# Attention of a transformer block: where the batches of maxima stand among the value products, where the additions follow, how often a modulation step comes, and what is held in SyncE's order

## The chip, the cores and the metric

The kernel runs on one core of one Trainium2 chip. The time is the device time of one execution in microseconds (us). Three runs of the kernel before gave 3038.39, 3041.65 and 3044.37 us, a median of 3041.65.

## What is computed

The reference is one layer of a diffusion backbone over 2048 latent tokens and 256 context tokens, all in float32: normalised and modulated input, a combined input projection, attention and a gated branch, a merge with an output projection, and a feed-forward part. The change touches the attention alone. There are 8 query heads and 2 key heads of 64 numbers, and each query reads 2304 keys (18 tiles of 128: two of context, sixteen of latent tokens).

```
def attend(q, k, v):
    s = jnp.einsum('bkgqd,bknd->bkgqn', q, k, preferred_element_type=jnp.float32)
    p = jax.nn.softmax(s, axis=-1).astype(v.dtype)
    return jnp.einsum('bkgqn,bknd->bkgqd', p, v)
```

## The kernel before, in words

**Units.** The attention (`attend`, L1119) goes through 16 units. A unit is a block of 512 queries (`b`, four of them) and a pair of heads (`p`, four of them). Units are numbered 0 to 15 here.

**What a unit needs.** Softmax is done with the maximum of each query subtracted. So before a unit's scores, its maxima have to be known: `maxima` (L2064) multiplies the queries' high halves with all keys, and VectorE reduces each 128x512 result to a column (L2084 for context keys, L2089 for the others). One call of `maxima(3)` is called a batch here: three steps, each of which fills two banks of PSUM and has two reduces. `reference` (L2093) takes the maximum over all key tiles. `leading` (L2100) turns the result into rows on TensorE (L2104), copies them on ScalarE (L2106) and sends them with eight transfers on SyncE's queue (L2109) into the first row of the operand `qb`, so that the product that follows subtracts the maximum. `cast` (L2052) and `remainder` (L2058) split the queries of a later unit into two parts; the second is two subtractions on VectorE (L2061).

**The order within a unit.** A unit's 18 key tiles are three groups of six (`GROUP`), `gi` 0, 1, 2; the text calls the work of one pass of this loop a block. For each key tile two products of scores are made for two heads (`first`, L2123, and `second`, L2142), and ScalarE takes their exponential out of PSUM (L2146) into the buffers `p2` (eight of them) and `t4`. Then come the first batch of maxima of a later unit, the value products of the group before (`pend`, `values`, L2149, the product in L2156), and the second batch. In blocks 0 and 1 the batches are of the next unit, in block 2 of the one after it. `values` also adds the exponentials up for the softmax's sum: key tiles 2, 4, 8 and 14 on VectorE (L2169), the others on GpSimd (L2172). `leave` (L2176) copies a finished output out of PSUM (L2180), `join` (L2183) adds the two sums (L2186), `sums` (L2193) sums over the partitions with a product with ones (L2199) and `inverse` (L2209) makes the reciprocal.

**What is done beside it.** `mod_part` (L352) makes one of the modulation vectors in steps of two rows of weights, on VectorE (L386, L390), in buffers of the tag `raw`; after each half of the vector a product with ones (L417) and two instructions of VectorE finish it. It is advanced three times a unit from unit 1 on, at the fifth key tile of each group. In the last unit `late` (`br_inputs`, L1188) loads eight inputs of the branch merge, four of one branch (`gm_d`) and four of the attention (`at_d`), and splits each of them, one a key tile: a load into one of three `raw` buffers (L1198), for the attention's also a load of the inverse sums (L1202) and a product with them on VectorE (L1217), a cast on ScalarE (L149) and a subtraction on VectorE (L153).

**What sets the order.** A scheduler places the instructions of each engine. In `attend` the instructions of TensorE and VectorE keep the order in which the code is written (`self.fixed`, read by `order`). ScalarE's, GpSimd's and SyncE's do not, save that buffers of one tag are first written in the written order, and save what `self.loads` holds, a list of stretches in which SyncE's transfers keep the written order; before, nothing of the attention is in it. PSUM has eight banks, all of one tag. A unit's output holds one from its first value product to `leave`, and the rest turn among scores, maxima and sums.

Of the kernel before, what the change touches and what calls it, by code (L numbers as in the profile page):

```python
# [29 lines left out]
TB = 512  # L30
# [34 lines left out]
GROUP = 6  # L65
# [4 lines left out]
class Kern:  # L70
# [1048 lines left out]
    def attend(self, units, late, mod):  # L1119
        self.psum({"b": 8})  # L1120
        begin = self.here()
        pend = []
        for i, u in enumerate(units):
            at = lambda n: units[n] if 0 <= n < len(units) else None
            nxt, far, old, older = at(i + 1), at(i + 2), at(i - 1), at(i - 2)
            for gi, g in enumerate(range(0, NKT, GROUP)):
                group = range(g, g + GROUP)
                step = nxt if gi < 2 else far
                for j in group:
                    u.first(j)  # L1130
                    u.second(j)
                    if j % GROUP == 2 and far and gi == 0:
                        far.load()
                    if j % GROUP == 4 and nxt and gi == 2:
                        nxt.leading()
                    if not nxt:
                        next(late, None)
                    elif i and j % GROUP == 4:
                        next(mod, None)
                if step:  # L1140
                    step.maxima(3)
                for f in pend:
                    f()
                if gi == 1 and far:
                    far.cast()
                if gi == 2 and old:
                    old.sums()
                if step:
                    step.maxima(3)
                if gi == 0:  # L1150
                    if older:
                        older.inverse()
                if gi == 2 and far:
                    far.remainder()
                if gi == 1:
                    if nxt:
                        nxt.reference()
                    if old:
                        old.join()
                pend = [lambda u=u, j=j: u.values(j) for j in group]  # L1160
            pend.append(u.leave)
        for _ in mod:
            pass
        for f in pend[:-1]:
            f()
        units[-2].inverse()
        units[-1].join([self.sb("raw", [TB]) for _ in range(2)])
        self.fixed.append(range(begin, self.here()))
# [865 lines left out]
class Unit:  # L2034
# [114 lines left out]
    def values(self, j):  # L2149
        k, nc = self.k, self.nc  # L2150
        c, i, _ = self.keys(j)
        pt, whole = self.pts.pop(j)
        if j == 0:
            self.o = k.bank([TB])
        for h in range(2):
            nc.tensor.matmul(  # L2156
                self.o[h * HD : (h + 1) * HD, :], k.V[c][:, i, self.kv * HD : (self.kv + 1) * HD],
                pt[h], start=j == 0, stop=j == NKT - 1,
            )
        e = j in (LAST_ON_VECTOR if self.last else ON_VECTOR)  # L2160
        old = self.acc.get(e)
        if old is None:
            self.acc[e] = whole
            return
        if e not in self.own:
            self.own.add(e)
            self.acc[e] = k.sb("ac", [2, TB])
        if e:
            nc.vector.tensor_tensor(out=self.acc[e], in0=old, in1=whole, op=ALU.add)  # L2169
        else:  # L2170
            for h in range(2):
                nc.gpsimd.tensor_tensor(  # L2172
                    out=self.acc[e][:, h], in0=old[:, h], in1=pt[h], op=ALU.add
                )
# [90 lines left out]
```

## Time and profile before

| | us |
|---|---|
| median of three runs | 3041.65 |
| the profiled execution, its own time | 3039.84 |
| its span, first to last instruction | 3038.1 |
| TensorE busy | 2957.5 (97% of the span) |
| VectorE busy | 2095.2 (69%) |
| ScalarE busy | 1438.3 (47%) |
| GpSimd busy | 657.0 (22%) |

The granted clock of TensorE is 0.989 of full speed on average over the execution. Line numbers of the profile are those of the kernel before. Engines are named PE (matmuls), PEld (weight loads, which run beside the matmuls), DVE (VectorE), ACT (ScalarE), POOL (GpSimd) and SP (SyncE). A matmul's end is modelled, and matmuls overlap, so the distance from one start to the next tells more than a row's own length. A matmul with float32 operands counts as two records.

### The profile page before, as it was taken

To read this page: it belongs to the slowest core of one execution; us is meant where nothing else is said; L and a number is where in the kernel's file an instruction comes from. 1 tells how busy PE (TensorE), PEld (TensorE's weight loads), DVE (VectorE), ACT (ScalarE), POOL (GpSimd) and SP (SyncE) were. 2 spreads that over 40 slices of the span, in tenths; PEclk is the share of its full clock that TensorE was granted. 3 is DMA by queue.
4 is the path that set the end of the run, shared out by engine and by line. 5 is a ranking of instruction groups with operands and counts; after the bars stand their busy time and mean duration, and the time that the engine had idled before them with its cause. 6 is when DMAs were issued, how large, how long until landed. Compare 5 with 4: busy or idle time off the path is not lost.

```text
span 3038.1 us, 37873 instructions
## 1 busy us (share of the span) xinstructions
PE 2957.5 (97%) x13325; PEld 2232.8 (73%) x13325; DVE 2095.2 (69%) x3007; ACT 1438.3 (47%) x2334; POOL 657.0 (22%) x470
## 2 busy tenths in 40 slices
PE   7989999998999999999999989999999999999999
PEld 4878888875555555555888878888887888888887
DVE  4867477876788877787655588776676666654555
ACT  5645765663545454454222254444454344444442
POOL 0000000000898898886222200000000000000000
PEclk9999999999999999999999999999999999999999
DMA  8686657654111000005767558888876544448554
GB/s 292 198 267 199 206 189 223 205 182 135 47 45 43 25 19 22 15 15 163 236 208 212 176 173 312 310 299 299 264 240 222 194 152 153 149 148 285 208 206 155
DMA packets 385439, 538.59 MB, mean 177 GB/s; under 512 B 37904, under 2 KB 196800, under 8 KB 385248
## 3 DMA queue, kind: packets, MB, share of 16 engines
q1 hardware_dynamic: 372880, 515.44, 51.4%
q10 hardware_dynamic: 12368, 20.73, 1.8%
q8 instruction: 105, 1.72, 0.2%
q14 instruction: 86, 0.70, 0.1%
HBM read 371.89 MB, written 164.10 MB: 176 GB/s over the span
## 4 chain that ended last, share of the span: by engine, by line
PE 83%; DVE 6%; DMA 5%; ACT 3%; issue 2%; SPq 1%; ACTq 0%; POOL 0%; DVEq 0%; POOLq 0%
PE b L1587 14%; PE b L1589 14%; PE b L1588 14%; PE b L2156 8%; PE b L2123 5%; PE b L2142 4%; PE b L182 4%; PE b L183 4%; PE b L184 4%; PE b L2078 3%; PE a L1587 3%; PE a L1588 3%; PE a L1589 3%; PE b L188 1%; DMA f<-t_d 1%
## 5 line engine op out<-in xcount | busy, mean ns | idle before, releaser
L2089 DVE TENSOR_REDUCE ts<-b 128x1 f32<-128x512 f32 x512 | 314.7, 681 | 94.5 <-PE b L2078 94.2
L2172 POOL TENSOR_TENSOR ac<-ac,p 128x512 f32<-128x512 f32 x214 | 296.0, 1415 | 55.3 <-ACT p L2146 55.3
L1703 DVE TENSOR_TENSOR b<-b,b 128x1024 fp32r<-128x1024 f32 x170 | 200.8, 1221 | 136.5 <-ACT b L1702 136.2
L1702 ACT CAST b<-b 128x1024 fp32r<-128x1024 f32 x170 | 170.7, 1051 | 223.2 <-PE b L1589 98.8
L2146 ACT ACTIVATE p<-b 128x512 f32<-128x512 f32 x384 | 197.5, 611 | 159.4 <-PE b L2142 92.6
L1588 PE MATMUL b<-b,b 128*128 128x512 f32 x680 | 265.3, 390 | 2.8 <-DVE b L1703 2.7
L1587 PE MATMUL b<-b,b 128*128 128x512 f32 x680 | 266.1, 391 | 1.6 <-DVE f L1724 1.4
L1589 PE MATMUL b<-b,b 128*128 128x512 f32 x680 | 264.7, 389 | 0.0
L2172 POOL TENSOR_TENSOR ac<-ac,t 128x512 f32<-128x512 f32 x152 | 221.8, 1488 | 0.0
L2172 POOL TENSOR_TENSOR ac<-p,p 128x512 f32<-128x512 f32 x32 | 47.9, 1517 | 772.4 <-ACT p L2146 772.4
L2123 PE MATMUL b<-h,h 128*128 128x512 f32 x576 | 202.6, 421 | 2.2 <-DVE ts L2089 1.0
L2142 PE MATMUL b<-h,h 128*128 128x512 f32 x576 | 180.9, 396 | 0.0
L2156 PE MATMUL b<-p,h 128*64 128x512 f32 x768 | 175.3, 598 | 0.9 <-ACT p L2146 0.9
L1588 PE MATMUL b<-hb,b 128*128 128x512 f32 x446 | 173.8, 390 | 0.0
L1597 DVE TENSOR_TENSOR f<-f,b 128x512 f32<-128x512 f32 x160 | 109.2, 682 | 78.8 <-issue 45.2
L1587 PE MATMUL b<-hb,b 128*128 128x512 f32 x415 | 161.6, 389 | 0.0
L1589 PE MATMUL b<-hb,b 128*128 128x512 f32 x415 | 161.3, 389 | 0.0
L2123 PEld LDWEIGHTS b<-h,h 128*128 128x128 f32 x576 | 107.2, 190 | 63.7 <-DVE ts L2089 23.2
L1588 PEld LDWEIGHTS b<-b,b 128*128 128x128 f32 x680 | 127.6, 188 | 31.3 <-DVE b L1703 4.7
L1587 PEld LDWEIGHTS b<-b,b 128*128 128x128 f32 x680 | 127.6, 188 | 29.5 <-ACT b L1702 2.3
L1589 PEld LDWEIGHTS b<-b,b 128*128 128x128 f32 x680 | 127.7, 188 | 26.4
L1587 PE MATMUL a<-f,h 128*128 128x384 f32 (+1 forms) x320 | 119.3, 377 | 13.5 <-ACT f L634 5.9
(434 smaller groups left out, 7269.4 us busy)
## 6 DMA issues: line engine op xcount, KB each, us to landing
ao_d<-f SPq DMA_DIRECT2D x224, 256.0 KB
f<-in_w_ff SPq DMA_DIRECT2D x48, 1024.0 KB
b<-ao_d SPq DMA_DIRECT2D x85, 512.0 KB
b<-w2o_d SPq DMA_DIRECT2D x85, 512.0 KB
w2o_d<-f SPq DMA_DIRECT2D x112, 256.0 KB
f<-in_w_in SPq DMA_DIRECT2D x44, 512.0 KB
f<-x_d SPq DMA_DIRECT2D x64, 256.0 KB
hb<-ao_d SPq DMA_DIRECT2D x54, 256.0 KB
```

The lines of the kernel that those rows point to most:

```text
L182: mm(ps, sh, mh, start=start, stop=False)
L1587: mm(ps, wh, hh, start=start and k == 0, stop=False, skip_group_check=True)
L1588: mm(ps, wh, hl, start=False, stop=False, skip_group_check=True)
L1589: mm(ps, wl, hh, start=False, stop=k == len(w) - 1, skip_group_check=True)
L1702: nc.scalar.copy(h, f32(l))
L1703: nc.vector.tensor_tensor(out=l, in0=f32(l), in1=f32(h), op=ALU.subtract)
L2089: nc.vector.tensor_reduce(out=self.mx[:, t, h, c : c + 1], in_=ps[h], axis=AX.X, op=ALU.max)
L2123: self.nc.tensor.matmul(self.pts[j][h], k.KA[c][self.kv][:, ks], self.qa[h], start=True, stop=False, skip_group_check=True,)
L2142: self.nc.tensor.matmul(s, k.KB[c][self.kv][:, ks], self.qb[h], start=False, stop=True, skip_group_check=True,)
L2146: self.nc.scalar.activation(pt[h], s, AF.Exp)
L2156: nc.tensor.matmul(self.o[h * HD : (h + 1) * HD, :], k.V[c][:, i, self.kv * HD : (self.kv + 1) * HD], pt[h], start=j == 0, stop=j == NKT - 1,)
L2172: nc.gpsimd.tensor_tensor(out=self.acc[e][:, h], in0=old[:, h], in1=pt[h], op=ALU.add)
```

## The change

It moves work within `attend` and splits `values` in two; no product, reduce or exponential is added or removed.

- The value products of a group no longer stand in one run between the two batches. One key tile's products come ahead of the first batch, three tiles' between the batches, two behind the second.
- The additions, now `gather`, stand behind all of that in the written order, and `leave` stands ahead of them.
- A modulation step is taken once a unit, at the end of block 0 from unit 1 on, where it was taken three times.
- `leading` and every step of `late` are written within `ordered`, which puts their stretch on `self.loads`, so that SyncE keeps their transfers in the written order.
- Behind the last unit, each value product is followed by its addition as before.

```
+        def run(lo, hi):
+            for j in pend[lo:hi]:
+                owner.values(j)
+
+        def ordered(work):
+            at = self.here()
+            work()
+            self.loads.append(range(at, self.here()))
+
+        def gather():
+            for j in pend:
+                owner.gather(j)
...
-                        nxt.leading()
+                        ordered(nxt.leading)
                     if not nxt:
-                        next(late, None)
-                    elif i and j % GROUP == 4:
-                        next(mod, None)
+                        ordered(lambda: next(late, None))
+                owner = u if gi else old
+                run(0, 1)
                 if step:
                     step.maxima(3)
-                for f in pend:
-                    f()
+                run(1, 4)
                 if gi == 1 and far:
                     far.cast()
                 if gi == 2 and old:
                     old.sums()
                 if step:
                     step.maxima(3)
+                run(4, GROUP)
                 if gi == 0:
+                    if old:
+                        old.leave()
+                    u.o = self.bank([TB])
+                gather()
+                if gi == 0:
+                    if i:
+                        next(mod, None)
                     if older:
                         older.inverse()
...
     def values(self, j):
...
-        pt, whole = self.pts.pop(j)
-        if j == 0:
-            self.o = k.bank([TB])
+        pt, _ = self.pts[j]
         for h in range(2):
             nc.tensor.matmul(
                 self.o[h * HD : (h + 1) * HD, :], k.V[c][:, i, self.kv * HD : (self.kv + 1) * HD],
                 pt[h], start=j == 0, stop=j == NKT - 1,
             )
+
+    def gather(self, j):
+        k, nc = self.k, self.nc
+        pt, whole = self.pts.pop(j)
         e = j in (LAST_ON_VECTOR if self.last else ON_VECTOR)
```

Three places show what this does to the engines' orders. In the rows `b` is a bank of PSUM, `p` and `t` are exponentials, `h` are operands of scores and maxima, `ac` are the running sums. Lines shift by 22 to 24 in the changed kernel: scores are L2145 and L2164 there, maxima L2100, values L2176.

The first place is TensorE at the end of block 0 of unit 13, where the next scores begin. Before, from the last two value tiles on:

```order
L2156 MATMUL b_11866<-t_2658_11954,h_6809 64x512 x2
L2156 MATMUL b_11866<-t_2663_11975,h_6809 64x512 x2
L2078 MATMUL b_12158<-h_6803,h_11888 128x512
L2078 MATMUL b_12159<-h_6877,h_11889 128x512
L2078 MATMUL b_12164<-h_6797,h_11888 128x512
L2078 MATMUL b_12165<-h_6868,h_11889 128x512
L2078 MATMUL b_12170<-h_6799,h_11888 128x512
L2078 MATMUL b_12171<-h_6871,h_11889 128x512
L2123 MATMUL b_12180<-h_11506,h_6580 128x512
L2123 MATMUL b_12181<-h_11507,h_6580 128x512
```

And of the changed kernel, from the value tile ahead of the second batch on:

```order
L2176 MATMUL b_11779<-p_2655_11945,h_6809 64x512 x2
L2100 MATMUL b_12140<-h_6803,h_11875 128x512
L2100 MATMUL b_12141<-h_6877,h_11876 128x512
L2100 MATMUL b_12146<-h_6797,h_11875 128x512
L2100 MATMUL b_12147<-h_6868,h_11876 128x512
L2100 MATMUL b_12152<-h_6799,h_11875 128x512
L2100 MATMUL b_12153<-h_6871,h_11876 128x512
L2176 MATMUL b_11779<-t_2658_11954,h_6809 64x512 x2
L2176 MATMUL b_11779<-t_2663_11975,h_6809 64x512 x2
L2145 MATMUL b_12181<-h_11489,h_6580 128x512
L2145 MATMUL b_12182<-h_11490,h_6580 128x512
```

The second batch stood directly ahead of the scores; two value tiles stand between them now. In the same way one value tile now stands between the scores and the first batch.

The second place is VectorE in block 0 of unit 1 (`ts` are columns of maxima, `raw` the modulation's buffers). Before, from the last two reduces of the first batch on:

```order
L2089 TENSOR_REDUCE ts_7248<-b_7482 128x1
L2089 TENSOR_REDUCE ts_7248<-b_7483 128x1
L2169 TENSOR_TENSOR ac_7238<-ac_7238,p_1360_7291 128x1024
L2089 TENSOR_REDUCE ts_7248<-b_7514 128x1
L2089 TENSOR_REDUCE ts_7248<-b_7515 128x1
L2089 TENSOR_REDUCE ts_7248<-b_7520 128x1
L2089 TENSOR_REDUCE ts_7248<-b_7521 128x1
L2089 TENSOR_REDUCE ts_7248<-b_7526 128x1
L2089 TENSOR_REDUCE ts_7248<-b_7527 128x1
L390 SCALAR_TENSOR_TENSOR raw_7453<-raw_7577,silu,raw_7453 128x512
L390 SCALAR_TENSOR_TENSOR raw_7453<-raw_7579,silu,raw_7453 128x512
```

And of the changed kernel, in the same block, from the middle of the reduces of the second batch on:

```order
L2111 TENSOR_REDUCE ts_7235<-b_7494 128x1
L2111 TENSOR_REDUCE ts_7235<-b_7495 128x1
L2111 TENSOR_REDUCE ts_7235<-b_7500 128x1
L2111 TENSOR_REDUCE ts_7235<-b_7501 128x1
L2193 TENSOR_TENSOR ac_7263<-ac_7263,p_1360_7291 128x1024
L386 TENSOR_SCALAR raw_7525<-raw_7526,silu 128x512
L390 SCALAR_TENSOR_TENSOR raw_7525<-raw_7528,silu,raw_7525 128x512
L2111 TENSOR_REDUCE ts_7235<-b_7589 128x1
L2111 TENSOR_REDUCE ts_7235<-b_7590 128x1
```

The addition stood between the two batches' reduces and stands behind both now; the twelve reduces of a block follow each other. A modulation step stood ahead of every block's first reduces; now it follows the addition of block 0 alone, ahead of block 1's reduces.

The third place is ScalarE in the last unit, from the end of block 0's exponentials to block 1's (`in` are the split branch inputs). Before, with the fifth, sixth and seventh of the eight casts:

```order
L2146 ACTIVATE t_2905_12845<-b_12841 128x512
L2146 ACTIVATE t_2905_12845<-b_12842 128x512
L149 CAST in_12856<-raw_12832 128x512
L2180 COPY t_2910_12883<-b_12628 128x512
L149 CAST in_12901<-raw_12850 128x512
L2181 DMA at_d_105<-t_2910_12883 128x512
L2146 ACTIVATE p_2913_12890<-b_12886 128x512
L2146 ACTIVATE p_2913_12890<-b_12887 128x512
L2146 ACTIVATE p_2920_12909<-b_12905 128x512
L2146 ACTIVATE p_2920_12909<-b_12906 128x512
L149 CAST in_12920<-raw_12895 128x512
```

And of the changed kernel, with the fourth, fifth and sixth:

```order
L149 CAST in_12837<-raw_12817 128x512
L2168 ACTIVATE t_2905_12845<-b_12841 128x512
L2168 ACTIVATE t_2905_12845<-b_12842 128x512
L149 CAST in_12856<-raw_12832 128x512
L2204 COPY t_2910_12872<-b_12545 128x512
L2205 DMA at_d_105<-t_2910_12872 128x512
L2168 ACTIVATE p_2914_12891<-b_12887 128x512
L2168 ACTIVATE p_2914_12891<-b_12888 128x512
L149 CAST in_12902<-raw_12850 128x512
L2168 ACTIVATE p_2921_12910<-b_12906 128x512
L2168 ACTIVATE p_2921_12910<-b_12907 128x512
L2168 ACTIVATE p_2928_12929<-b_12925 128x512
```

Before, one cast is placed far ahead in unit 4 and two ahead of the last unit's exponentials, and the fourth as the last unit begins. In the changed kernel the first stands there, the second, third and fourth stand among the twelve exponentials of block 0, and two exponentials of block 1 have moved ahead of the sixth cast. On SyncE's queue, the loads of the first three branch inputs and of two inverse sums stood among the transfers of units 4 and 5; all eight inputs stand behind the last unit's leading rows now.

More of the change, by code (lines that the diff above doesn't have):

```diff
@@ L1121, in attend @@
         begin = self.here()
-        pend = []
+        old, pend = None, []
+        def run(lo, hi):
[8 more added lines that the diff above has]
+                owner.gather(j)
         for i, u in enumerate(units):
@@ L1159, in attend @@
                         old.join()
-                pend = [lambda u=u, j=j: u.values(j) for j in group]
-            pend.append(u.leave)
+                pend = list(group)
         for _ in mod:
             pass
-        for f in pend[:-1]:
-            f()
+        owner = units[-1]
+        for j in pend:
+            owner.values(j)
+            owner.gather(j)
         units[-2].inverse()
```

## The prediction

> **What bounds the kernel now.** I read the page first: the span, the busy shares and the chain.
>
> ```profile
> span 3038.1 us, 37873 instructions
> ...
> PE 2957.5 (97%) x13325; PEld 2232.8 (73%) x13325; DVE 2095.2 (69%) x3007; ACT 1438.3 (47%) x2334; POOL 657.0 (22%) x470
> ...
> PE 83%; DVE 6%; DMA 5%; ACT 3%; issue 2%; SPq 1%; ACTq 0%; POOL 0%; DVEq 0%; POOLq 0%
> ```
>
> TensorE is the bound, so an edit is worth what it takes out of, or puts into, TensorE's own sequence. The change lies in the attention, so the waits come next, for 770 to 1410 us (who waited, for whom, us in total, times, longest).
>
> ```profile
> PEld b L2123 <- DVE ts L2089: 22.3, 68, 0.7
> PEld b L2078 <- DVE ac L2169: 20.3, 25, 0.8
> PEld b L2078 <- ACT t L2146: 18.6, 54, 0.4
> ```
>
> Scores (L2123) wait for VectorE to reduce a bank of maxima. Maxima (L2078) wait for ScalarE to finish the exponentials, or, by the second row, for VectorE. These are idle times of the weight loader, which is ahead of the matmuls: they name the waits, and their size has to come from the timeline. So third, TensorE in one undisturbed unit, from 1006.32 to 1047.19 (start, length, engine, line, count; the gap to the next row's start is what a row really costs).
>
> ```profile
> 1006.32 0.88 PE L2123 MATMUL b<-h,h 128*128 128x512 f32 x2
> ...
> 1012.44 1.34 PE L2078 MATMUL b<-h,h 64*128 64x512 f32 x6
> 1013.71 3.65 PE L2156 MATMUL b<-p,h 128*64 128x512 f32 x16
> 1017.20 1.89 PE L2156 MATMUL b<-t,h 128*64 128x512 f32 x8
> 1019.01 0.96 PE L2078 MATMUL b<-h,h 64*128 64x512 f32 x6
> 1019.91 0.73 PE L2123 MATMUL b<-h,h 128*128 128x512 f32 x2
> ...
> 1025.57 0.96 PE L2078 MATMUL b<-h,h 64*128 64x512 f32 x6
> 1026.52 3.65 PE L2156 MATMUL b<-p,h 128*64 128x512 f32 x16
> ...
> 1031.82 0.96 PE L2078 MATMUL b<-h,h 64*128 64x512 f32 x6
> 1032.71 0.88 PE L2123 MATMUL b<-h,h 128*128 128x512 f32 x2
> ...
> 1037.83 0.27 PE L2104 MATMUL b<-ident,ts 128*8 128x128 f32 x1
> ...
> 1038.95 1.25 PE L2078 MATMUL b<-h,h 64*128 64x256 f32 x10
> 1040.13 3.65 PE L2156 MATMUL b<-p,h 128*64 128x512 f32 x16
> ...
> 1045.33 1.03 PE L2199 MATMUL b<-ac,ones 128*64 128x512 f32 x4
> ...
> 1047.19 0.88 PE L2123 MATMUL b<-h,h 128*128 128x512 f32 x2
> ```
>
> A unit is three blocks (0, 1, 2, the groups of six key tiles), each of scores, first batch, values, second batch. Scores take 6.12, 5.66 and 6.24 us, the first batch 1.27, 0.95 and 1.18, the values 5.30, 5.30 and 5.20 (then sums, 0.96), the second batch 0.90. The same work takes 5.66 and 0.95 in block 1, where no output bank is held and all eight banks turn. So blocks 0 and 2 hold stalls, and block 1 none: 0.46 + 0.32 in block 0. Block 2's scores hold the transpose of the leading rows too, (L2104, a record of 0.27 that partly lies under its neighbours; I take 0.15), so 0.43; of its first batch, which has four narrow pairs, I take 0.2 as stall, between nothing and block 0's 0.32. That is 1.41 us a unit, all that the placing of the batches can win.
>
> **The change part by part.** *The batches between values.* A first batch then starts behind one value tile, a second behind three more, and the last two value tiles stand between it and the next scores. What a split of the values costs is in the same rows. Twelve pairs of value records take 5.30 when maxima follow and 5.20 when sums of the same array shape follow: leaving the shape costs 0.10. Eight pairs at the head take 3.49 (1013.71 to 1017.20); with 5.20 for twelve that is 0.43 a pair and 0.07 for entering. Each extra run of values therefore costs 0.17, and there are two: 0.34. A batch followed by values takes 0.95 and one followed by scores 0.90, and the second batch becomes the former. With the rounding of the rows this is 0.36 a block (0.33 to 0.39), 1.08 a unit. [...]
>
> Does every stall go? By banks: ScalarE's twelve exponentials run from about 1 us behind the start of the scores.
>
> ```profile
> 1020.97 4.03 ACT L2146 ACTIVATE p<-b 128x512 f32<-128x512 f32 x8 [1.25 <-PE b L2142]
> ```
>
> One each (4.03 - 0.6) / 7 = 0.49 us, the eleventh ends near 1.06 + 10 x 0.49 + 0.65 = 6.6. The third pair of the first batch needs that bank: before at 5.66 + 0.6 = 6.3, so it waits 0.3; after at 5.66 + 1.03 + 0.6 = 7.3. That stall goes. For the second batch and the scores, VectorE decides.
>
> ```profile
> 1009.55 3.38 DVE L2061 TENSOR_TENSOR h<-t,h 128x512 fp32r<-128x512 f32 x2
> 1012.97 3.68 DVE L2089 TENSOR_REDUCE ts<-b 128x1 f32<-128x512 f32 x6
> 1016.57 2.27 DVE L2169 TENSOR_TENSOR ac<-ac,p 128x1024 f32<-128x1024 f32 x1
> ...
> 1036.17 1.30 DVE L2186 TENSOR_TENSOR ac<-ac,ac 128x1024 f32<-128x1024 f32 x1
> ...
> 1043.09 1.55 DVE L2169 TENSOR_TENSOR ac<-ac,p 128x1024 f32<-128x1024 f32 x1
> ```
>
> Six reduces take 3.60 (1012.97 to 1016.57) and begin 0.53 behind their batch. After, the second batch starts 0.95 + 2.75 = 3.70 behind the first and its third pair needs the fifth bank of the first, free at 0.53 + 5 x 0.60 = 3.53, against 3.70 + 0.6: 0.7 us of slack. The addition now comes behind the second batch: 4.13 for the reduces, 1.55 to 2.27 for the addition, then in block 2 the two remainders, 3.38: 9.06 to 9.78. The next first batch starts at 0.95 + 1.89 + 5.66 + 1.03 = 9.53 and its reduces would start at 10.06. VectorE is free 0.3 us earlier at the least. So I let all stalls go, and the bounds for what stays are nothing and 0.2 us a block. The scores need the sixth bank of the second batch 5.7 behind it, and it is free at 4.2. An exponential that reuses the buffer of a late addition is the seventh of its block, some 6.9 behind the second batch, against 6.4 for the end of the addition: no wait.
>
> Sum for a steady unit: 1.08 - 1.41 = -0.33. Units 1 to 13 have it in full, 13 x -0.33 = -4.3. In units 0 and 14 it about cancels (two blocks each).
>
> *One modulation step a unit.* Steps now run in units 1 to 4, three a unit, between the batches.
>
> ```profile
> 798.40 0.89 PE L2123 MATMUL b<-h,h 128*128 128x512 f32 x2
> ...
> 965.45 0.89 PE L2123 MATMUL b<-h,h 128*128 128x512 f32 x2
> ...
> L390 DVE SCALAR_TENSOR_TENSOR raw<-raw,silu,raw 128x512 f32<-128x512 f32 x14 | 23.9, 1708 | 0.3
> ...
> L417 PE MATMUL b<-raw,ones 128*128 128x512 f32 x4 | 2.0, 593 | 0.0
> ```
>
> Units 1 to 4 take (965.45 - 798.40) / 4 = 41.76, the steady one 40.87: 4 x 0.89 = 3.6 us more. Two products with ones (L417) are in that, two records each, at most 2 x 0.9 us, and they only move to units 6 and 12: 1.8 us are won. After, a step is two instructions of 1.71 behind block 0's addition, 4.13 + 2.27 + 3.42 = 9.8 against the same 10.06, so it is covered; without the cover it would cost what the step exceeds it by, a few tenths in eight units.
>
> *The fixed order of leading rows and branch loads.* In steady units SyncE sends the same transfers in the same order, and leading rows go out where they did. In the last unit it matters.
>
> ```profile
> 1366.36 4.93 SPq L2109 DMA_DIRECT2D h<-t  x8
> ...
> 1374.34 0.63 ACT L149 CAST in<-raw 128x512 fp32r<-128x512 f32 x1 [1.32 <-DMA raw<-gm_d]
> ...
> 1387.17 0.62 ACT L149 CAST in<-raw 128x512 fp32r<-128x512 f32 x1 [2.64 <-DVE raw L1217]
> ...
> 1383.15 2.29 DVE L2169 TENSOR_TENSOR ac<-ac,p 128x1024 f32<-128x1024 f32 x1
> 1385.36 1.77 DVE L1217 TENSOR_TENSOR raw<-raw,gx 128x512 f32<-128x512 f32 x1
> ...
> 1391.72 3.65 PE L2156 MATMUL b<-p,h 128*64 128x512 f32 x16 [0.93 <-ACT p L2146]
> ```
>
> Before, three of the eight branch inputs are loaded many units ahead and are cast and split before the last unit's scores; the fourth lands at 1374.34. After, all eight stand behind the last leading rows in SyncE's order, so the first of them lands where the fourth did, and four casts stand between block 0's exponentials. On the clock of before: splits of about 1.7 us follow casts at 1374.3, 1378, 1379.5 and 1381; the first product with the inverse sums (L1217) ends at 85.8 instead of 77.8; cast, split, addition (2.29) and the second product bring the cast that stood at 1387.17 to about 1392. Two exponentials now go ahead of it, the third waits. The scores of block 1 need four to get their twelfth bank, so values start near 1394.4 instead of 1391.72: +2.6 us. Bounds: 0, where the chain closes as early as today, and 4.5, nearly the whole 5 us of the cast's delay.
>
> Sum: -4.3 - 1.8 + 2.6 = -3.5. The profiled execution took 3039.84 (span 3038.1 and 1.7 around it), which gives 3036.3; it lies 1.8 below the median of the runs, and on the median of 3041.65 it is 3038.1.
>
> **The rivals.** A measurement of this kernel can tell about 0.2%, 6.1 us, from no change.
> 1. The last unit loses nothing: its exponentials already waited 2.2 us in block 1 before, and a wait that overlaps another is free. Then -6.1 us, 3035.5, and less where a split costs 0.33. Against it: the static order of ScalarE, where casts stand ahead of exponentials. Chance 0.28, and this is faster, if barely.
> 2. VectorE is late (slower). The addition and the two remainders, or the modulation step, are pushed together behind the second batch of blocks 0 and 2, while GpSimd adds the whole time. If they lengthen as the addition does between 1.55 and 2.27, by half, the chain of block 2 becomes 4.13 + 2.3 + 5.0 = 11.4, 1.4 later than the reduces should start; beyond the 0.7 of slack TensorE waits 0.67 in 26 blocks, 17 us, and the time is 3055. It decides from 1.1 us of lateness, where 26 x 0.37 = 9.6 turn -3.5 into +6.1. For it: the additions' spread. Against: the remainders at 3.38 already ran beside GpSimd. [...] Chance 0.13.
> 3. The stalls go only by half (the banks come round in another order than the one in which they come free): 0.7 a unit is not won, +9.1, and the time is 3047, within 0.2%. Chance 0.11.
>
> **How the numbers follow.** My forecast has 0.48. Its own range is 3035 to 3042. The forecast and rival 3 are within 0.2% (0.59), less 0.02 that the forecast's spread passes to faster and 0.01 that rival 3 passes to slower: same 0.56, faster 0.30, slower 0.14. The likeliest time is 3038.1. The range takes rival 1 with runs that spread by 3 us below it (3032) and rival 3 nearly (3046), and leaves out rival 2.
>
> **What would show it.** Right: units of about 40.5 us from unit 1 to 13 without long ones at 1 to 4; every block's scores at 5.66, first batches at 0.95, values in three runs of 1.0, 2.7 and 1.9; no scores or maxima waiting for VectorE among the waits; block 1 slower than before, blocks 0 and 2 faster; the last unit about 2.6 us longer, with ScalarE's casts waiting for L1217's product. Wrong: maxima of the second batch waiting for the first batch's reduces, value runs that cost more than 0.17 at their ends, or a last unit as short as now.

## The result, and the profile after

The changed kernel took 3031.86 us (median of 12 runs, 3026.64 to 3037.5), the kernel before 3041.55 (12 runs, 3037.63 to 3046.75). The ratio is 0.9969, 95% interval 0.9961 to 0.9977: 9.7 us faster, 0.31%. The forecast was 3038.1, so it is 6.2 us too high; the time lies right at the lower edge of the range of 3032 to 3046. Faster by over 0.2% had 0.30, no change 0.56.

The profiled execution took 3034.03 us. The attention in it, from the first score to the first product of the branch merge, went from 655.92 us to 648.96. What follows it is the same code and stayed within 2.2 us.

TensorE of the changed kernel in one undisturbed unit, 1037.15 to 1077.32, with the starts of units 1 and 5 ahead of it; scores are L2145, maxima L2100, values L2176:

```profile
795.24 0.73 PE L2145 MATMUL b<-h,h 128*128 128x512 f32 x2
...
955.94 0.72 PE L2145 MATMUL b<-h,h 128*128 128x512 f32 x2
...
1037.15 0.73 PE L2145 MATMUL b<-h,h 128*128 128x512 f32 x2
...
1050.21 0.73 PE L2145 MATMUL b<-h,h 128*128 128x512 f32 x2
...
1055.87 1.08 PE L2176 MATMUL b<-p,h 128*64 128x512 f32 x4
1056.88 0.96 PE L2100 MATMUL b<-h,h 64*128 64x512 f32 x6
1057.78 2.79 PE L2176 MATMUL b<-p,h 128*64 128x512 f32 x12
1060.50 0.96 PE L2100 MATMUL b<-h,h 64*128 64x512 f32 x6
1061.39 1.94 PE L2176 MATMUL b<-t,h 128*64 128x512 f32 x8
1063.26 0.73 PE L2145 MATMUL b<-h,h 128*128 128x512 f32 x2
...
1069.07 1.08 PE L2176 MATMUL b<-p,h 128*64 128x512 f32 x4
...
1077.32 0.73 PE L2145 MATMUL b<-h,h 128*128 128x512 f32 x2
```

From start to start, block 1 is scores 5.66, one value tile 1.01, first batch 0.90, three tiles 2.72, second batch 0.89, two tiles 1.87: 13.05 us, with no stall. Block 0 is the same to 0.01 (1037.15 to 1050.21), and block 2 takes 14.06 with its transpose and sums. The unit takes 40.18 where it took 40.87. Units 1 to 4, with the modulation, take (955.94 - 795.24) / 4 = 40.18 as well, where they took 41.76.

The waits from 770 to 1400 us show why idle times of the weight loader (PEld) aren't read as a price:

```profile
PEld b L2100 <- ACT t L2168: 34.2, 44, 0.8
...
PEld b L2145 <- DVE ts L2111: 23.7, 32, 0.8
```

Both sums are larger than before (18.6 and 22.3), and yet no matmul behind them starts late: the loader waits inside the time that the value products fill.

VectorE in the same blocks has as little to spare as predicted, or a little more (0.3 to 1.0 us there). Its row of reduces, addition (L2193) and remainders (L2083) runs until 1.22 us before the next reduces:

```profile
1075.09 3.68 DVE L2111 TENSOR_REDUCE ts<-b 128x1 f32<-128x512 f32 x6 [0.80 <-PE b L2100]
1078.69 1.22 DVE L2193 TENSOR_TENSOR ac<-ac,p 128x1024 f32<-128x1024 f32 x1
1079.83 3.48 DVE L2083 TENSOR_TENSOR h<-t,h 128x512 fp32r<-128x512 f32 x2
1084.53 0.69 DVE L2111 TENSOR_REDUCE ts<-b 128x1 f32<-128x512 f32 x1 [1.22 <-PE b L2100]
```

Once in this execution, in unit 11, that slack was not enough. The addition beside GpSimd's (POOL) took 5.26 us, and the exponential that reuses its buffer waited:

```profile
1195.86 5.02 POOL L2196 TENSOR_TENSOR ac<-ac,t 128x512 f32<-128x512 f32 x4
...
1199.20 5.26 DVE L2193 TENSOR_TENSOR ac<-ac,p 128x1024 f32<-128x1024 f32 x1
...
1200.82 2.56 POOL L2196 TENSOR_TENSOR ac<-p,p 128x512 f32<-128x512 f32 x2
...
1204.55 1.09 ACT L2168 ACTIVATE p<-b 128x512 f32<-128x512 f32 x2 [2.61 <-DVE ac L2193]
```

The first batch of that block took 3.05 instead of 0.89 and the values behind it 4.42 instead of 2.73, for the granted clock fell as well (0.79 on average from 1204 to 1212, 0.52 from 1208.0 to 1211.4): 3.85 us for one slow addition. GpSimd's additions, of some 1.25 us each, follow each other without a break until 1203.38, and VectorE's ends 1.08 us after them; the shortest of its kind in this run took 1.21. What held the addition for 5.26 us is not shown.

In the last unit, ScalarE's casts (L149) wait for the products with the inverse sums (L1239), and TensorE for the exponentials behind them:

```profile
1363.55 0.62 ACT L149 CAST in<-raw 128x512 fp32r<-128x512 f32 x1 [3.41 <-DMA raw<-gm_d]
...
1374.95 0.62 ACT L149 CAST in<-raw 128x512 fp32r<-128x512 f32 x1 [3.37 <-DVE raw L1239]
...
1379.48 0.62 ACT L149 CAST in<-raw 128x512 fp32r<-128x512 f32 x1 [1.85 <-DVE raw L1239]
...
1380.65 0.99 PE L2145 MATMUL b<-h,h 128*128 128x512 f32 x2 [2.01 <-ACT p L2168]
...
1382.06 5.28 PE L2176 MATMUL b<-p,h 128*64 128x512 f32 x16
```

The last row, sixteen records that take 3.65 elsewhere, is slow for another reason. Busy time of PE, PEld, DVE, ACT and POOL in two stretches, then the granted clock:

```profile
1382.00:1385.40 3.40, 3.40 (x9) 1.01 (x10) 1.91 (x3) 3.40 (x8) 0.93 (x1) 0.51 0.04 14
1385.40:1388.80 3.40, 3.40 (x18) 0.98 (x14) 3.40 (x3) 0.92 (x2) 3.40 (x3) 1.00 0.00 0
```

From 1.4 us behind the end of the 2.01 us gap the clock was half for 3.4 us, which costs 5.28 - 3.65 = 1.63 us more. The last unit took 44.85 us (before, 41.71).

### The profile page after: what moved, and what is told of

Same layout as the page of the kernel before. It is cut to its first block, busy times and chain, and to the rows that moved or that the text cites. A ratio compares the mean times of both kernels' runs of the same rounds, so it can differ in the third digit from the quotient of the medians.

```text
span 3032.2 us, 37907 instructions
## 1 busy us (share of the span) xinstructions
PE 2951.8 (97%) x13325; PEld 2221.2 (73%) x13325; DVE 2088.1 (69%) x3007; ACT 1434.0 (47%) x2334; POOL 650.6 (21%) x470
## 4 chain that ended last, share of the span: by engine, by line
PE 85%; DVE 5%; DMA 5%; ACT 3%; issue 2%; SPq 0%; POOL 0%; ACTq 0%; DVEq 0%; POOLq 0%
PE b L1609 14%; PE b L1611 14%; PE b L1610 14%; PE b L2176 8%; PE b L2145 4%; PE b L2164 4%; PE b L182 4%; PE b L183 4%; PE b L184 4%; PE a L1609 3%; PE a L1610 3%; PE a L1611 3%; PE b L2100 3%; PE b L188 1%; DMA m<-in_w_in 1%
## 5 line engine op out<-in xcount | busy, mean ns | idle before, releaser
L2196 POOL TENSOR_TENSOR ac<-ac,p 128x512 f32<-128x512 f32 x214 | 306.4, 1465 | 55.8 <-ACT p L2168 55.8
L2196 POOL TENSOR_TENSOR ac<-ac,t 128x512 f32<-128x512 f32 x152 | 204.1, 1375 | 0.0
L2145 PE MATMUL b<-h,h 128*128 128x512 f32 x576 | 188.1, 406 | 3.3 <-ACT p L2168 2.6
L2176 PE MATMUL b<-p,h 128*64 128x512 f32 x768 | 188.1, 613 | 0.0
L2164 PE MATMUL b<-h,h 128*128 128x512 f32 x576 | 179.1, 392 | 0.0
L2145 PEld LDWEIGHTS b<-h,h 128*128 128x128 f32 x576 | 104.2, 189 | 64.5 <-DVE ts L2111 25.4
```

Source lines behind the costliest of these rows:

```text
L2145: self.nc.tensor.matmul(self.pts[j][h], k.KA[c][self.kv][:, ks], self.qa[h], start=True, stop=False, skip_group_check=True,)
L2164: self.nc.tensor.matmul(s, k.KB[c][self.kv][:, ks], self.qb[h], start=False, stop=True, skip_group_check=True,)
L2176: nc.tensor.matmul(self.o[h * HD : (h + 1) * HD, :], k.V[c][:, i, self.kv * HD : (self.kv + 1) * HD], pt[h], start=j == 0, stop=j == NKT - 1,)
L2196: nc.gpsimd.tensor_tensor(out=self.acc[e][:, h], in0=old[:, h], in1=pt[h], op=ALU.add)
```

## The experiments

All against the kernel before on the same chip. The attention and the units are from the start times of TensorE in the profiled execution; a steady unit is the median of units 5 to 13.

| run | median | ratio (95%) | attention | steady unit | units 1-4 | last unit |
|---|---|---|---|---|---|---|
| before | 3041.55 | | 655.92 | 40.87 | 41.76 | 41.71 |
| the change | 3031.86 | 0.9969 (0.9961-0.9977) | 648.96 | 40.19 | 40.18 | 44.85 |
| e1_batches | 3032.62 | 0.9968 (0.9956-0.9979) | 648.59 | 40.35 | 41.30 | 43.55 |
| e2_batches_adds | 3036.24 | 0.9979 (0.9970-0.9989) | 650.05 | 40.17 | 42.14 | 43.83 |
| e3_adds | 3134.87 | 1.0302 (1.0289-1.0316) | 746.83 | 47.96 | 47.00 | 40.89 |
| e6_second | 3043.15 | 1.0005 (0.9994-1.0016) | 655.67 | 40.98 | 40.96 | 44.55 |
| e7_first | 3060.91 | 1.0063 (1.0049-1.0077) | 672.85 | 42.17 | 42.35 | 42.87 |
| e8_mod | 3038.96 | 0.9991 (0.9981-1.0001) | 653.68 | 40.89 | 40.89 | 41.67 |
| e4_late_free | 3029.09 | 0.9958 (0.9946-0.9971) | 647.80 | 40.18 | 40.18 | 43.87 |
| e5_late_early | 3032.72 | 0.9968 (0.9957-0.9980) | 646.95 | 40.19 | 40.18 | 46.40 |
| e9_spread | 3027.31 | 0.9953 (0.9940-0.9965) | 639.45 | 40.18 | 40.18 | 38.99 |
| e10_adds_in | 3033.50 | 0.9978 (0.9968-0.9987) | 648.16 | 40.52 | 40.42 | 44.54 |
| e11_both | 3030.09 | 0.9963 (0.9951-0.9976) | 642.69 | 40.51 | 40.44 | 39.04 |
| e12_six | 3077.25 | 1.0121 (1.0108-1.0135) | 690.25 | 43.27 | 43.27 | 44.49 |

**The change taken apart.** e1_batches has the batches' new places alone. Against the changed kernel the additions go back into the runs of values, the modulation back to three steps a unit, and nothing is held in order:

```
             for j in pend[lo:hi]:
                 owner.values(j)
+                owner.gather(j)
...
-                gather()
```

> The changed kernel's places of the two batches alone: additions stand with their value tile again, modulation three steps a unit, nothing ordered on SyncE. Theory (the batches' places win, the additions behind them are the condition): in block 0 the addition of 1.2 to 2.3 us stands between the two batches' reduces, so the second batch's banks come free late and block 0's scores behind it stall by 0 to 0.9 us, 0.4 on average; a steady unit is 40.4 to 40.9 us (changed kernel 40.18, before 40.87), units 1 to 4 are longer by about 1 us each from modulation, the last unit is about 41.7; in all 2 to 6 us below before, that is 3036 to 3040. Rival (the additions' place alone makes the gain): the unit is at 41 us or more, the time that of before or above.

It reached 3032.62, within the noise as much as the whole change, and below what was expected. Most of the gain, 0.52 of the 0.69 us of a steady unit, comes from the batches' places.

e2_batches_adds is the same with the additions behind, as in the change.

> The batches' places and the additions behind them, but modulation three steps a unit as before and nothing ordered on SyncE. Theory: steady units at 40.18 as in the changed kernel, units 1 to 4 some 0.5 to 1.5 us longer each, units 6 and 12 shorter by 0.9 each, the last unit as before (41.7 in place of 43 to 45): in all within 2 us of the changed kernel, 3031 to 3034. Rival (modulation makes most of the gain): 3036 or more.

The steady unit improved from 40.35 to 40.17, but units 1 to 4 became longer, 42.14 against 41.30. Three modulation steps a unit cost 0.89 us a unit before, 0.95 in e1_batches, and 1.97 behind the late additions. The expectation missed this: the two edits share VectorE's slack. The time, 3036.24, is the one that the rival gave, but not for its reason, since modulation alone makes a small part of the gain (e8_mod, below).

e3_adds has the additions behind and the batches in their old places:

```
-                run(0, 1)
                 if step:
                     step.maxima(3)
-                run(1, 4)
+                run(0, GROUP)
...
-                run(4, GROUP)
```

> The additions behind both batches' reduces, while the batches stand where they stood before, and modulation and SyncE as before. Theory: no stall of TensorE hangs on the additions there (VectorE is early for the second batch either way): steady units 40.8 to 41.0, the time of before within 2 us. Rival (the additions' place alone makes the gain): steady units near 40.2 to 40.4 and 6 to 9 us below before.

It is 94 us slower, where the same time as before was expected. VectorE, ScalarE and TensorE of this run in one block (values are L2174 here, additions L2191, exponentials L2166, maxima L2098):

```profile
1038.70 2.23 DVE L2191 TENSOR_TENSOR ac<-ac,p 128x1024 f32<-128x1024 f32 x1
...
1041.02 1.09 ACT L2166 ACTIVATE p<-b 128x512 f32<-128x512 f32 x2 [1.08 <-DVE ac L2191]
...
1041.59 2.05 PE L2098 MATMUL b<-h,h 64*128 64x512 f32 x5
1044.96 0.69 PE L2098 MATMUL b<-h,h 64*128 64x512 f32 x1 [1.32 <-DVE ts L2109]
1045.58 5.09 PE L2174 MATMUL b<-p,h 128*64 128x512 f32 x16
```

The scores follow the second batch at once, so the seventh exponential needs the buffer of the addition 1.87 us earlier than in the change, and waits 1.08. The exponentials end late, the first batch lacks banks, its reduces come behind the remainders, and a second wait of 1.32 follows, with half the clock behind it (the granted clock was 0.51 from 1045.0 to 1048.4). This is near the second rival's mechanism: VectorE is late because the addition and the remainders follow each other. What it holds up first is an exponential's buffer, by 1.08 us; in the change that buffer is free in time.

e6_second moves the second batch alone (`run(0, 4)` behind the first batch), e7_first the first alone (`run(0, 1)` ahead of it, `run(1, GROUP)` behind); all else is as in the change.

> The changed kernel with the second batch alone between values: the first batch stands directly behind the scores again and four value tiles stand between the batches. Theory (each batch wins its own stall): first batches of 1.28, 0.95 and 1.17 us as before, scores without stall, one value run less: a steady unit of 40.4, 0.23 above the changed kernel, 3 us in all: 3035. Rival (what counts is that the batches are apart, not that each has values ahead of what waits): 40.2 or less.

> The changed kernel with the first batch alone between values: the second batch stands directly ahead of the next scores again. Theory (each batch wins its own stall): scores of 6.1 and 6.25 us in blocks 0 and 2 as before, first batches of 0.9: a steady unit of 40.6, 0.4 above the changed kernel, 5 us in all: 3037. Rival (the first batch makes the gain): 40.2 or less.

Both missed: 40.98 and 42.17 us a unit. In e6_second the scores are free of stalls (5.67), and the first batch, directly behind them, takes 1.38, 1.28 and 1.25 (L2099; values are L2175):

```profile
1044.58 1.45 PE L2099 MATMUL b<-h,h 64*128 64x512 f32 x6
1045.96 3.65 PE L2175 MATMUL b<-p,h 128*64 128x512 f32 x16
...
1059.26 3.65 PE L2175 MATMUL b<-p,h 128*64 128x512 f32 x16 [0.20 <-DVE ts L2110]
```

In block 0 this is the wait for the exponentials' banks that the prediction put at 0.3. In block 1, which had none before, the profile names another: the first value product waits 0.20 us for a reduce. The code takes the output's bank earlier now, at the end of block 0; that this is the reason is not shown. In e7_first the second batch stands ahead of the scores, which stall as before (6.09), and VectorE, held by the addition and remainders (L2082), is late for the first batch:

```profile
1055.12 3.46 DVE L2082 TENSOR_TENSOR h<-t,h 128x512 fp32r<-128x512 f32 x2
1058.51 3.67 DVE L2110 TENSOR_REDUCE ts<-b 128x1 f32<-128x512 f32 x6
```

The reduces start at 1058.51 behind a first batch that began at 1056.84. The two places don't add up, then: either one alone, with the additions behind, loses what it wins, or more.

e8_mod is the kernel before with the modulation step once a unit, behind block 0.

> The kernel before with one modulation step a unit at the end of block 0 and nothing else. Theory: steady units unchanged at 40.9, units 1 to 4 at 40.9 instead of 41.76, units 6 and 12 longer by 0.9: 1 to 3 us below before. Rival (modulation makes most of the gain): 5 us or more below before.

Units 1 to 4 came down to the steady 40.89, and the attention by 2.2 us. Of these, 0.9 lie in unit 0, where no modulation step runs; units 1 to 13 won about 1.4, since units 6 and 12, where the products with ones stand now, grew by 1.1 each. The time agrees with that, but its interval just reaches no change.

**The last unit.** e4_late_free is the change with the branch loads not held in order, so that two casts come ahead of the last unit; e5_late_early begins the branch inputs in block 2 of unit 14.

```
-                    if not nxt:
+                    if not nxt or (not far and gi == 2):
                         ordered(lambda: next(late, None))
```

> The changed kernel, with the loads of the last unit's branch inputs no longer held in SyncE's written order; the leading rows stay held. Theory (the fixed order puts four casts and their splits into the last unit's blocks): three inputs are loaded and split ahead again, the last unit falls from 43.2 us (44.84 less a dip of the granted clock) to about 41.7, and the time by 1 to 2 us to 3030. Rival (the last unit's time is set by the inverse sums and the additions, not by the order): the last unit stays within 0.5 us.

> The changed kernel, with the branch inputs begun six key tiles earlier, in block 2 of unit 14, where VectorE has no maxima. Theory: block 0 and block 1 of the last unit lose their waits (6.44 and 9.19 us of scores become about 5.7 each), unit 14 grows by at most 0.5: 3 to 4 us below the changed kernel, 3028. Rival: the loads wait in unit 14 as they do in unit 15 (the leading rows' eight transfers hold SyncE for 4.9 us in that very block), the chain moves there and the gain is under 1 us.

Without the order the last unit takes 43.87, 1.0 less, which is neither the 41.7 of the theory nor within the rival's 0.5; the ratio's interval holds the change's ratio, so the time alone doesn't show it. It loses for another reason than the change. On SyncE's queue a branch load stands ahead of the leading rows, which begin to go out at 1361.29 (in the change at 1355.57), and the scores wait for them:

```profile
1360.85 0.35 SPq L1220 DMA_DIRECT2D raw<-gm_d  x1
1361.29 4.97 SPq L2131 DMA_DIRECT2D h<-t  x8
...
1367.36 0.79 PE L2164 MATMUL b<-h,h 128*128 128x512 f32 x1 [1.96 <-DMA h<-t]
```

The granted clock is 0.50 from 1367.3 to 1370.6. The same wait stands in e1_batches (1.92) and e2_batches_adds (1.95), which hold nothing in SyncE's order. So the order spares one loss and brings another, and its price of 1.0 us is the difference.

Beginning earlier did not help, 46.40:

```profile
1362.58 0.47 PE L2164 MATMUL b<-h,h 128*128 128x512 f32 x1 [0.70 <-DMA h<-t]
...
1380.35 1.28 PE L2145 MATMUL b<-h,h 128*128 128x512 f32 x2 [2.42 <-ACT p L2168]
```

The scores wait for the leading rows (0.70), which SyncE sends among the branch loads now, and exponentials still stand behind casts that wait for VectorE (2.42), as the rival had it. The clock is at half for twice as long as in the change (0.50 on average from 1379.2 to 1385.9).

e9_spread takes one branch input a block, over the last three units:

```
-                    if not nxt:
+                    if i >= len(units) - 3 and j % GROUP == 4:
                         ordered(lambda: next(late, None))
```

> The changed kernel with the branch inputs taken one step a block over the last three units, where all stood in the last. Theory (the last unit's 44.85 us hold about 5 us in which exponentials stand behind casts that wait for VectorE): the last unit near 39.5, units 13 and 14 at most 0.5 longer each, attention 644, time 3027, ratio 0.995. Rival (the splits and products, 1.0 to 1.8 us each, meet VectorE's narrow slack in units 13 and 14, whose reduces come late): 1 to 2.5 us more in each of them, nothing won, 3031 or more.

The first score of each of the last unit's blocks, and the merge's first product:

```profile
1356.80 0.73 PE L2145 MATMUL b<-h,h 128*128 128x512 f32 x2
...
1367.77 0.74 PE L2145 MATMUL b<-h,h 128*128 128x512 f32 x2
...
1378.78 0.74 PE L2145 MATMUL b<-h,h 128*128 128x512 f32 x2
...
1395.79 2.13 PE L1330 MATMUL b<-in,bw 128*128 128x512 f32 x8
```

The last unit takes 38.99 us, with no stall and no fall of the clock; unit 14 grew by 0.24. This is the best version of all, 3027.31. Its interval still touches that of the change, but its place is seen in the profile: 5.9 of the change's last 44.85 us were the casts and what followed them.

**Where the additions stand, and what a split costs.** e10_adds_in is the change with each addition behind its own value tile (the diff of e1_batches alone), e11_both that with the branch inputs spread.

> The changed kernel with each addition written behind its own value tile again, all else as changed. Theory (the batches' places make the gain; the additions behind add only the risk that one of them is late): unit 40.2 to 40.4, no stall in unit 11, attention 645 to 647, time 3028 to 3030, ratio 0.996. Rival (a VectorE addition between the reduces delays the second batch's banks, so that the additions behind are worth something): unit 40.6 to 40.9, 3035 or more.

> The edits of the two runs before it together. If they add up: attention 641 to 643, time 3024 to 3026, ratio 0.9945. If either uses the slack that the other needs: 3028 or more.

The unit is 40.52 in e10_adds_in, between the two expectations, and 40.51 in e11_both. VectorE and TensorE at the end of a block 0 of e10_adds_in:

```profile
1091.49 1.84 DVE L2193 TENSOR_TENSOR ac<-ac,p 128x1024 f32<-128x1024 f32 x1
1093.26 3.67 DVE L2111 TENSOR_REDUCE ts<-b 128x1 f32<-128x512 f32 x6
```

```profile
1090.98 0.97 PE L2100 MATMUL b<-h,h 64*128 64x512 f32 x6
...
1094.79 0.90 PE L2145 MATMUL b<-h,h 128*128 128x512 f32 x2
```

The addition holds the second batch's reduces until 2.3 us behind its start, and the third pair of scores waits 0.3 (its row 0.90, a plain one 0.62). So the additions behind win 0.3 us a unit here, and 0.18 in e2_batches_adds against e1_batches, where no modulation step runs in these units. Whether that is worth more than the rare slow one isn't settled. e9_spread and e11_both differ in this alone, with 639.45 against 642.69 in the attention and medians of 3027.31 against 3030.09; but the profiled execution of e9_spread holds no slow addition and is the fastest of its five runs (3022.19 to 3030.85), and the intervals of the two ratios overlap. In the attention e11_both is what adding up predicted (641 to 643); its time is not (3024 to 3026).

e12_six cuts a block's maxima into five batches and the values into six runs:

```
                 run(0, 1)
-                if step:
-                    step.maxima(3)
-                run(1, 4)
+                for k in range(3):
+                    if step:
+                        step.maxima(1)
+                    run(1 + k, 2 + k)
...
                 if step:
-                    step.maxima(3)
-                run(4, GROUP)
+                    step.maxima(1)
+                run(4, 5)
+                if step:
+                    step.maxima(2)
+                run(5, GROUP)
```

> The changed kernel with the same maxima in five smaller batches and so the values of a block in six runs where there were three; nothing else is moved. If a further run of values costs what the changed kernel's block 1 shows, (13.05 - 12.80) / 2 = 0.125 us: 0.375 more a block, a unit of 41.3 and a time of 3046. If it costs the 0.18 of the prediction (0.36 for two): 0.54 more a block, a unit of 41.8 and 3053.

Neither held; the unit takes 43.27. TensorE in one block (values L2180, maxima L2104):

```profile
1084.10 1.08 PE L2180 MATMUL b<-p,h 128*64 128x512 f32 x4
1085.11 0.49 PE L2104 MATMUL b<-h,h 64*128 64x512 f32 x2
1085.54 1.08 PE L2180 MATMUL b<-p,h 128*64 128x512 f32 x4
...
1090.85 0.73 PE L2104 MATMUL b<-h,h 64*128 64x512 f32 x4
1091.51 1.08 PE L2180 MATMUL b<-t,h 128*64 128x512 f32 x4
1092.52 0.74 PE L2149 MATMUL b<-h,h 128*128 128x512 f32 x2
```

A run of one value tile takes 1.01, of two 1.87, of three 2.73, of six 5.30: 0.86 a tile and 0.15 a run. A batch of one step takes 0.43, of two 0.66, of three 0.89: 0.23 a step and 0.19 a batch. Three further runs and three further batches are 3 x (0.15 + 0.19) = 1.02 a block, and the block grew from 13.05 to 14.08. Both expectations counted the runs and forgot the batches. The change itself added two runs and no batch.

## Why the prediction was right or wrong, step by step

| step | predicted | measured |
|---|---|---|
| stalls that go, a unit | 1.41 | 1.44 (0.69 won + 3 x 0.25 paid, with block 1's 0.25 taken for each block) |
| the split, a block | 0.36 | 0.25 (block 1: 12.80 to 13.05) |
| a steady unit | -0.33 | -0.69 |
| units 1 to 13 by this | -4.3 | -9.0 |
| modulation | -1.8 | -1.9 (4 x 0.89 less 2 x 0.85, by which units 6 and 12 are longer now) |
| last unit | +2.6 | +3.1, of which 1.6 half clock |
| units 0 and 14 | 0 | -2.1 (granted clock in unit 0: 0.89 before, 0.95 after, which makes about 2.5 by my estimate) and -0.8 |

**The step that failed** is the price of a split: "A batch followed by values takes 0.95 and one followed by scores 0.90, and the second batch becomes the former." Between values a batch takes 0.89, whichever comes next. It was the batch behind the scores that took 0.95, and that place is gone. So the batches gave 0.06 a block instead of costing 0.05; the two further runs cost 2 x 0.15, near the predicted 0.34. The difference is 0.11 a block, 0.33 a unit, 4.3 us in 13 units. It is the largest of the terms that come back unit after unit; with 0.25 in the prediction's own sum, 3033.8 would have come out, which is already "faster" and no longer "no change". That the range reaches down to 3032 at all is rival 1's doing, which did not happen; so it is luck that the time lies at its edge.

**The stalls** went in full, as forecast, and rival 3 (half of them stay) is out: blocks 0, 1 and 2 have none. But the argument was thinner than it read. It took each stall by itself, and e6_second and e7_first show that one batch alone gains nothing. One sign did not hold as written: scores still stand among the waits for VectorE (23.7 us), though it is only the weight loader that waits.

**Rival 2** (VectorE late) decided the change's fate more nearly than its 0.13 said. Where the values behind the scores and the 1.87 us between the second batch and the scores are both missing, e3_adds is 94 us slower; where the 1.87 alone are missing, e7_first is 19 us slower. In the change it struck once in the profiled execution (3.85 us in unit 11), and once in that of e4_late_free; the profiles of e2_batches_adds, e5_late_early and e9_spread, with the same order in a steady unit, have none. How often it strikes over many runs stays open, and so does how much of the spread of 3026.6 to 3037.5 it makes.

**The modulation** was right in direction and size. Its worth depends on the additions: by itself about 1.4 us (units 1 to 13 of e8_mod), but with the additions behind, three steps would have cost 1.97 a unit in units 1 to 4.

**The last unit** was right in mechanism and place: casts wait for L1239's product, exponentials behind them, scores behind those (2.01). Its size was right by luck: the waits beyond those before are 1.5 in place of the predicted 2.6, and 1.6 of half clock, which the prediction had not thought of, stand in for the rest. The prediction also charged the fixed order with the whole loss. e4_late_free, without it, still takes 2.2 more than before (43.87 against 41.71), with late leading rows in place of late casts. Rival 1 (nothing lost) is out, and e9_spread shows that the loss wasn't needed.

The sum by the profile is -9.0 - 1.9 + 3.1 - 2.9 + 3.9 (unit 11) = -6.8, against -6.96 seen in the attention. The medians differ by 9.7; without the stall of unit 11 the sum would be -10.7. The two profiles are single draws, and the rest isn't settled.

## What to carry to other kernels

A price for cutting a run in two is taken from rows with the same neighbours as after the cut, and counted for every kind of run that becomes more numerous; here a row from another place, the batch behind the scores, gave it too high (0.95, where 0.89 came out). Additions moved behind the reduces were harmless but once in the change, where VectorE has 1.22 us to spare (9.7 us faster), and ruinous in e3_adds (94 us slower), by what stood between them and what reads or reuses their buffers, so edits that share such slack are costed together and not one by one. Feeders of a next stage that ride on a busy engine belong spread over earlier, steady stages, where e9_spread took them at 0.24 us more in unit 14 and left the last unit 5.9 shorter.

## What the runs showed of the hardware

- The clock fell to half for 3.4 us, or twice that (0.50 from 1379.2 to 1385.9 in e5_late_early), at gaps of TensorE of 1.3 to 2.4 us: in the change behind 2.01 (0.51 from 1382.0 to 1385.4), in e3_adds behind 1.32 (0.51 from 1045.0 to 1048.4; nine such waits, 11.9 us in all, stand there between 770 and 1400). There one late reduce cost its 1.32 and then 5.09 - 3.65 = 1.44 more in the sixteen value records behind it. In unit 11 of the change the clock fell behind a slow batch with no gap over 0.5. The longest gap in units 1 to 15 of any run, 3.17 us in the last unit of e7_first, brought no fall; the granted clock there is 1.00, and the sixteen records behind the gap take 3.65 as elsewhere:

```profile
1407.65 3.65 PE L2175 MATMUL b<-p,h 128*64 128x512 f32 x16 [3.17 <-ACT p L2167]
```

- So the length of a gap alone doesn't decide, and what does is not shown here.
- An addition of 128x1024 on VectorE took 1.21 to 2.31 us in the change and 5.26 once, and 1.21 to 2.32 before.
- Each run of value products (128*64 in the rows) cost 0.15 us beside 0.86 a tile, and each batch of maxima (64*128) 0.19 beside 0.23 a step (e12_six).
